# A table of biases built in the first half-step, a norm's small products moved into products, and half 0's squares ordered behind an inverse root

## The chip, the cores and the metric

The kernel runs on one core of one Trainium2 chip. The core has TensorE (PE, matrix products), VectorE (DVE), ScalarE (ACT), GpSimd (POOL) and SyncE (SP, which issues transfers); 16 DMA engines move data between HBM and the on-chip memory. The metric is the device time of one execution in microseconds (us), lower is better; a time given for a kernel is the median of several runs. A profile is taken from one further execution.

## The reference

One step of a decoder layer on 544 tokens of width 1024 (512 of a prompt, 8 samples of 4): a SwiGLU half-step, a mixer of two groups of heads (RWKV-7 and differential attention), and a second SwiGLU half-step, each between two norms. The attention adds a bias that depends on the distance of two tokens alone, looked up in a table of 32 buckets for 4 heads.

```python
def layer(x, l, shift0, wkv0, attend, P):
    g = P['norm_gains'][l]
    h = x + 0.5 * rms_norm(swiglu(rms_norm(x, g[0], NORM_EPS), P['ff1_in'][l], P['ff1_out'][l]), g[1], NORM_EPS)
    m, k, v, wkv, shift = mixer(rms_norm(h, g[2], NORM_EPS), l, shift0, wkv0, attend, P)
    h = h + rms_norm(m, g[3], NORM_EPS)
    h = h + 0.5 * rms_norm(swiglu(rms_norm(h, g[4], NORM_EPS), P['ff2_in'][l], P['ff2_out'][l]), g[5], NORM_EPS)
    return h, k, v, wkv, shift
...
    s = jnp.einsum('bqhmd,bkhmd->bhmqk', q, k).astype(jnp.float32) * (A_QK_DIM ** -0.5)
    s = s + bias[None, :, None]
```

## The kernel before

The tokens lie along the free dimension in two halves of 272 (half 0 and half 1, index s), the 1024 features in 8 blocks of 128 partitions (KB). A product in fp32 is made of three products in a faster type: every matrix is kept as a high part and a low part, and the three are high by high, low of x by high of w, high of x by low of w. `weights` (L110 to L125) brings one block of weights: SyncE loads it into a buffer named wraw (there are three, shared by all loads of this kind), ScalarE copies the high part whi (L118), and the low part wlo is either a subtraction on VectorE (L124) or, with `added`, a negated copy on ScalarE (L121) and a transfer on GpSimd's queue that adds the weights onto it (L122).

`dot` multiplies a block of weights with one half of x: for eight blocks k the two products with whi (L144, L145), then eight with wlo (L153). `opening` (L345 to L373) makes the first products of a stage: for half 0 with `dot`, then for half 1, two weights at a time, with `mm3` (L129, L130, L131). While these run, the stage before is being closed: `close_half` (L293 to L327) makes the residual h of a half (L301, L302 on VectorE), splits it into xh (ScalarE, L279) and xl (VectorE, L281), the operands of the products, and adds up its squares for the next norm (ScalarE L259, VectorE L260). The norm itself is a list of steps: small products that sum the squares (L191), an inverse root of 9 small VectorE instructions (L216 to L226), small products that spread it over the partitions (L238), and for the next norm a copy of it, rpre (L291), by which results are scaled (for the mixer, L741). `dot` and `opening` issue one step each when their products are through, so `norm` and `ends`, the two lists, set where the small products stand in TensorE's order.

The scheduler of the tile layer orders instructions on each engine by priority; `tc.issue_after(ins)` sets one behind another, and `tc.high_priority()` sets it ahead of others that are ready.

The mixer's opening is followed by the gates: a Tanh and a Sigmoid (L807, L808) on the first two projections, their split parts twh, twl, sgh, sgl, and small products with the weights lora (`gates`, L129 to L131 again). Then come four blocks b=0 to 3, each with three more weights and their products. Ahead of these, in the code, stands the table: L828 loads the buckets of 640 distances (oh), L832 multiplies them with the table of biases (tab), L833 negates the result into rb, L836 writes rb to memory, L839 writes it 128 times side by side (rb_d, 1280 KB). Both oh and rb are wraw buffers. The attention reads rb_d at L1130, 634 us into the run.

The half-steps go through 22 blocks of inner features in four groups. The first group opens with `opening` for blocks 0 and 1 and goes on with pairs of blocks from j = 2.

Of the kernel before, what the change touches and what calls it, by code (L numbers as in the profile page):

```python
# [9 lines left out]
FT = mybir.dt.float32  # L10
# [10 lines left out]
KB = DM // 128  # L21
# [31 lines left out]
def build(ctx, tc, A):  # L53
# [84 lines left out]

    def dot(ps, w, xs, k0=0, ins=None):

        n = len(xs)
        for k in range(n):
            hi, _ = wcols(w, k0 + k)
            T.matmul(ps, hi, xs[k][0], start=k == 0, stop=False)  # L144
            latest[0] = T.matmul(ps, hi, xs[k][1], start=False, stop=False).ins  # L145
        rest = norm and norm[0] is None
        if rest:
            norm.pop(0)
        elif norm:
            ins = norm_step(latest[0], norm)  # L150
        with after(ins):
            for k in range(n):
                latest[0] = T.matmul(ps, wcols(w, k0 + k)[1], xs[k][0], start=False, stop=k == n - 1).ins  # L153
        if rest and norm and norm[0] is not None:
            norm_step(latest[0], norm)
# [21 lines left out]
    def xbank():  # L177
        return px.tile([128, 512], FT, name="pb")

    turn, last, latest = [0], [None], [None]  # L180

    def acc_tile():
        turn[0] += 1
# [19 lines left out]
    def inv_sqrt(pt, n, scale=1.0, eps=None, least=None, y=None):  # L203


        if y is None:
            v, y, t = [wk.tile([128, n], FT, name=nm, bufs=3, padded_shape=[128, 24]) for nm in ("rv", "ry", "rt")]
        else:
            v, t = [wk.tile([128, n], FT, name=nm, tag="sq") for nm in ("wv", "wt")]
        src, dst = pt[:], v  # L210
        if len(src.shape) == 2:
            src = src[:, :n]
        else:
            dst = v.rearrange("p (b j e) -> p b j e", j=src.shape[2], e=src.shape[3])
        if least is None:
            V.tensor_scalar(dst, src, 0.5 * scale, 0.5 * eps, op0=OP.mult, op1=OP.add)  # L216
        else:
            V.tensor_scalar(dst, src, least, 0.5, op0=OP.max, op1=OP.mult)
        V.tensor_scalar(y.bitcast(I32), v.bitcast(I32), -0.5, MAGIC, op0=OP.mult, op1=OP.add)
        V.tensor_tensor(t, v, y, op=OP.mult)  # L220
        V.tensor_tensor(t, t, y, op=OP.mult)
        V.scalar_tensor_tensor(t, t, -5 / 3, t, op0=OP.add, op1=OP.mult)
        V.scalar_tensor_tensor(y, t, 1.25, y, op0=OP.add, op1=OP.mult)
        V.tensor_tensor(t, v, y, op=OP.mult)
        V.scalar_tensor_tensor(t, t, -3.375, y, op0=OP.mult, op1=OP.mult)
        V.scalar_tensor_tensor(y, t, 2.25, y, op0=OP.add, op1=OP.mult)  # L226
        return y

    def spread(y, e, bank=bank):
# [65 lines left out]
    def close_half(h, s, y, sq, gcol, pre=None, xp=None, spill=None, out=None):  # L295

        drain()

        def residual(r, m):
            t = wk.tile([128, HALF], FT, name="pn")  # L300
            V.scalar_tensor_tensor(t, y[s][m], gcol[:, m:m + 1], r, op0=OP.mult, op1=OP.mult)  # L301
            (G if out is not None and m in (0, 2, 4) else V).tensor_tensor(h[s][:, m], h[s][:, m], t, op=OP.add)  # L302
            if out is not None and (m % 2 or m == KB - 2):
                q = m if m >= KB - 2 else m - 1
                nc.sync.dma_start(out[s, :, q:m + 1], h[s][:, q:m + 1])
            if pre is not None:
                pre.split(xp, h, s, m)
            if spill is not None and m % 2:
                nc.scalar.dma_start(spill[s, :, m - 1:m + 1], h[s][:, m - 1:m + 1])

        def steps(r):
            for m in range(KB):
                with (tc.high_priority() if s else ExitStack()):
                    residual(r, m)
                yield
            if pre is not None:
                for m in range(KB):
                    pre.sq[s].add(h[s][:, m])
                    yield

        if s == 1 and pre is not None:
            norm.extend((lambda _: inverses(sq), lambda iv: later.append(steps(spread(iv, 1))),
                         None, None, lambda _: inverses(pre.sq[0]), lambda iv: pre.scale(0, iv)))
            ends.extend((lambda _: inverses(pre.sq[1]), lambda iv: pre.scale(1, iv)))
        else:
            later.append(steps(rstd(sq)))
# [17 lines left out]
    def opening(ws, xs, take, n=4):  # L344


        for i, w in enumerate(ws):
            ps = acc_tile()
            dot(ps, w, xs[0])
            take(0, i, ps)  # L350
            tick(4)
        drain()
        for i in range(0, len(ws), n):
            banks = [acc_tile() if j < 3 else abank()[:, :HALF] for j in range(min(n, len(ws) - i))]
            for k in range(KB):
                for w, ps in zip(ws[i:i + n], banks):
                    latest[0] = mm3(ps, wcols(w, k), xs[1][k], k == 0, k == KB - 1)
                if norm and k == 2:
                    norm_step(latest[0], norm)
            if ends and i:  # L360
                norm_step(latest[0], ends)
            for j, ps in enumerate(banks):
                take(1, i + j, ps)
        norm.extend(ends)
        ends.clear()
# [59 lines left out]

        return sets, scaled(), mixtures()

    def ff(win, wout, pre, h, done, xp, end, lead=(), begin=None, ahead_of_end=None):
        with ExitStack() as st:
            pool = lambda n, to=st, **kw: to.enter_context(tc.tile_pool(name=n, bufs=1, reuse_waits="tile", **kw))  # L430
            yp, fa = pool("ffy"), pool("fa")
# [110 lines left out]
            for gi, (j0, j1) in enumerate(GROUPS):  # L542
                if gi == 0:
# [16 lines left out]
                    scaled_raw(0)  # L560
                    behind = [None, None]
                    for j in range(2, j1, 2):
                        ws = [[weights(win[i, n], 1024, added=begin is None and j == 2) for n in range(2)] for i in (j, j + 1)]
                        for s in range(2):
                            for both in ws:
                                pg, pu = acc_tile(), acc_tile()
# [91 lines left out]
        pre.scale(1)  # L658

    hd = dram.tile([2, 128, KB, HALF], FT, name="h_d")  # L660
    mix_in = Pre(2)
    mixp = []

# [11 lines left out]
    def ff1_end():  # L675
# [1 line left out]
        again(A["x"])  # L677

    ff(A["ff1_in"], A["ff1_out"], pre, h,
       lambda s, y, sq: close_half(h, s, y, sq, hgains[:, 1, :], mix_in, mixp[0], hd), xp, ff1_end, lead, begin, mix_weights)  # L680
    xs, rs = mix_in.xs, mix_in.rs
    h_stack.close()

# [139 lines left out]
            out.append(t)  # L823
        return out


    oh = wp.tile([33, NRB], FT, name="wraw", bufs=3)
    nc.sync.dma_start(oh, A["rbkt"])  # L828
    rb = wp.tile([AH, NRB], FT, name="wraw", bufs=3)
    for c0, c1 in ((0, 512), (512, NRB)):  # L830
        ps = abank()
        T.matmul(ps[:AH, :c1 - c0], tab, oh[:, c0:c1], start=True, stop=True)  # L832
        V.tensor_scalar(rb[:, c0:c1], ps[:AH, :c1 - c0], -1.0, None, op0=OP.mult)  # L833

    rb_1 = dram.tile([AH, NRB], FT, name="rb_1")
    nc.sync.dma_start(rb_1, rb)  # L836
    rb_d = dram.tile([128, AH * NRB], FT, name="rb_d")
    src = rb_1[0:1]
    nc.sync.dma_start(rb_d, bass.AP(tensor=src.tensor, offset=src.offset, ap=[[0, 128], [1, AH * NRB]]))  # L839
    for b in range(4):  # L840
        cat = pp.tile([128, NCH, 5, CH], FT, name="cat", bufs=2)
        if b:
# [794 lines left out]
```

## Time and profile before

| what | value |
|---|---|
| timed runs | 1208.91, 1209.03, 1210.56 us |
| median | 1209.03 us |
| profiled execution | 1214.19 us, its span 1212.4 us |
| granted TensorE clock, mean over the span | 0.982 |
| TensorE busy | 1173.4 us, 97% of the span |
| VectorE, ScalarE, GpSimd busy | 816.1, 587.9, 165.0 us |

The span is the time between the first and the last instruction in the record. The granted clock is the share of full speed that TensorE had. A busy share near 100% says that an engine nearly always has work, not that it works at full speed.

### The profile page before, as it was taken

What the parts mean: (1) busy time and instruction counts of PE and PEld (TensorE: products, weight loads), DVE (VectorE), ACT (ScalarE), POOL (GpSimd) and SP (SyncE); (2) the same over time, 40 slices, a digit from 0 to 9 for tenths busy, and PEclk for the clock granted to TensorE, in tenths of its full rate; (3) what the DMA queues carried; (4) which work ended last, traced back from release to release, by engine and by line L of the source; (5) the groups of instructions that cost most, each with busy time, mean ns of one, the idle gap of its engine ahead of it and who ended that gap; (6) DMA issues with size and microseconds to landing.
All of it is one profiled execution on the core that took longest, in us unless ns stands there. A gap on an engine that the chain in (4) does not pass through costs nothing. (4 is left out here: it accounts for less than half of the span.)

```text
span 1212.4 us, 25438 instructions
## 1 busy us (share of the span) xinstructions
PE 1173.4 (97%) x10020; PEld 1106.2 (91%) x10020; DVE 816.1 (67%) x1876; ACT 587.9 (48%) x1085; POOL 165.0 (14%) x227
## 2 busy tenths in 40 slices
PE   8999999999999979989999999999999999999996
PEld 8999999999999969989897645998999999999995
DVE  7794684865866657768525458785783766857856
ACT  6455552644645465543214446576455544625530
POOL 0001210110102055531000021101002110101001
PEclk8999999999999979999999899999999999999998
DMA  6328884875756277789426376663538985867532
GB/s 217 101 67 240 213 210 128 209 182 143 166 193 158 76 203 206 218 228 251 116 66 194 140 283 216 210 181 110 136 95 236 219 200 141 212 155 169 122 124 74
DMA packets 86349, 206.47 MB, mean 170 GB/s; under 512 B 9137, under 2 KB 20145, under 8 KB 84822
## 3 DMA queue, kind: packets, MB, share of 16 engines
q1 hardware_dynamic: 66150, 151.10, 37.4%
q0 software_dynamic: 17776, 49.29, 23.2%
q10 hardware_dynamic: 2304, 4.46, 1.0%
q8 instruction: 79, 1.29, 0.4%
q14 instruction: 40, 0.33, 0.1%
HBM read 187.17 MB, written 18.95 MB: 170 GB/s over the span
## 5 line engine op out<-in xcount | busy, mean ns | idle before, releaser
L118 ACT ACTIVATE whi<-wraw 128x1024 fp32r<-128x1024 f32 (+2 forms) x127 | 116.8, 923 | 166.8 <-PE mm L145 70.4
L144 PE MATMUL mm<-xh,whi 128*128 128x272 f32 x456 | 122.7, 299 | 11.5 <-ACT whi L118 7.7
L145 PE MATMUL mm<-xl,whi 128*128 128x272 f32 x456 | 121.3, 295 | 0.0
L124 DVE TENSOR_TENSOR wlo<-wraw,whi 128x1024 fp32r<-128x1024 f32 (+2 forms) x98 | 98.2, 1004 | 17.7 <-ACT whi L118 14.4
L144 PEld LDWEIGHTS mm<-xh,whi 128*128 128x128 f32 x456 | 88.7, 195 | 13.3 <-ACT whi L118 8.0
L463 POOL DMA_DIRECT2D t<-in_ff_in_dram x32 | 38.6, 1205 | 397.3 <-DMA t<-in_ff_in_dram 207.8
L145 PEld LDWEIGHTS mm<-xl,whi 128*128 128x128 f32 x456 | 88.8, 195 | 0.4 <-DVE xl L281 0.3
L509 DVE TENSOR_TENSOR ga<-pb,ga 128x272 f32<-128x272 f32 x140 | 61.1, 436 | 22.3 <-PE pb L498 20.1
L153 PE MATMUL mm<-xh,wlo 128*128 128x272 f32 x456 | 70.1, 293 | 1.4 <-DMA wlo<-in_ff_in_dram 1.4
L495 PE MATMUL pb<-sh,t1h 128*128 128x272 f32 x256 | 66.7, 288 | 0.0
L496 PE MATMUL pb<-sl,t1h 128*128 128x272 f32 x256 | 66.6, 287 | 0.0
L608 DVE TENSOR_TENSOR y<-mm,y 128x272 f32<-128x272 f32 x66 | 29.0, 440 | 54.9 <-PE mm L153 54.5
L153 PEld LDWEIGHTS mm<-xh,wlo 128*128 128x128 f32 x456 | 62.0, 191 | 2.2 <-DMA wlo<-in_ff_in_dram 1.8
L145 PE MATMUL mm<-hd1l,whi 128*128 128x272 f32 x242 | 62.7, 289 | 1.0 <-DVE hd1l L165 1.0
L145 PE MATMUL mm<-hd0l,whi 128*128 128x272 f32 x242 | 62.6, 288 | 0.0
L144 PE MATMUL mm<-hd0h,whi 128*128 128x272 f32 x242 | 62.2, 288 | 0.0
L144 PE MATMUL mm<-hd1h,whi 128*128 128x272 f32 x242 | 62.1, 289 | 0.0
L144 PE MATMUL pb<-xh,whi 128*128 128x272 f32 x232 | 60.9, 292 | 0.6 <-ACT whi L118 0.6
L145 PE MATMUL pb<-xl,whi 128*128 128x272 f32 x232 | 59.7, 288 | 0.0
L475 ACT ACTIVATE t1h<-t 128x1024 fp32r<-128x1024 f32 x32 | 33.9, 1061 | 52.6 <-issue 26.5
L495 PE MATMUL pb<-fa,whi 128*128 128x272 f32 x216 | 56.2, 288 | 0.0
L496 PE MATMUL pb<-fa,whi 128*128 128x272 f32 x216 | 56.2, 288 | 0.0
(508 smaller groups left out, 3621.0 us busy)
## 6 DMA issues: line engine op xcount, KB each, us to landing
wraw<-in_ff_in_dram SPq DMA_DIRECT2D x55, 512.0 KB, 5.3
wlo<-in_ff_in_dram POOLq DMA_DIRECT2D x36, 512.0 KB, 7.4
t<-in_ff_in_dram SPq DMA_DIRECT2D x64, 256.0 KB, 3.7
t<-in_ff_in_dram POOLq DMA_DIRECT2D x32, 512.0 KB, 5.9
wraw<-in_w_in_dram SPq DMA_DIRECT2D x26, 512.0 KB, 7.3
wlo<-in_w_in_dram POOLq DMA_DIRECT2D x25, 512.0 KB, 9.0
wraw<-in_ff_out_dram SPq DMA_DIRECT2D x32, 384.0 KB, 3.0
wraw<-in_ff_out_dram SPq DMA_DIRECT2D x32, 320.0 KB, 3.2
```

The source lines that it names most:

```text
L118: S.activation(hi, raw, AF.Copy)
L124: V.tensor_tensor(lo, raw, hi.bitcast(FT), op=OP.subtract)
L144: T.matmul(ps, hi, xs[k][0], start=k == 0, stop=False)
L145: latest[0] = T.matmul(ps, hi, xs[k][1], start=False, stop=False).ins
L153: latest[0] = T.matmul(ps, wcols(w, k0 + k)[1], xs[k][0], start=False, stop=k == n - 1).ins
L463: G.dma_start(t1, bass.AP(tensor=src.tensor, offset=src.offset, ap=[[1024, 128], [128 * 1024 + 512, 2], [1, 512]]), accum_op=OP.add)
L475: S.activation(hi, src, AF.Copy)
L495: T.matmul(ps, c, x[k][0], start=k == 0, stop=False)
L496: T.matmul(ps, c, x[k][1], start=False, stop=False)
L509: V.tensor_tensor(dst, p, q, op=op)
L608: V.tensor_tensor(y[s][m], ps, y[s][m], op=OP.add)
```

## The change

Four things change. The table is built by a function `distances`, called in the first half-step, with tiles of its own and its three transfers on GpSimd's queue. `dot` issues a step of a norm after the fourth of its eight blocks k, and sets the products after that behind the step; `opening` does the like for the list `ends`. Half 0's squares leave the steps of half 0 and are queued by the step that makes half 1's sums and root, behind the last instruction of that root. In the second half-step's first group the accumulating transfer makes the low parts of block 3 alone, no longer those of blocks 2 and 3.

```diff
     def dot(ps, w, xs, k0=0, ins=None):
-        n = len(xs)
-        for k in range(n):
-            hi, _ = wcols(w, k0 + k)
-            T.matmul(ps, hi, xs[k][0], start=k == 0, stop=False)
-            latest[0] = T.matmul(ps, hi, xs[k][1], start=False, stop=False).ins
+        n, then = len(xs), None
         rest = norm and norm[0] is None
         if rest:
             norm.pop(0)
-        elif norm:
-            ins = norm_step(latest[0], norm)
+        for k in range(n):
+            hi, _ = wcols(w, k0 + k)
+            with after(then):
+                T.matmul(ps, hi, xs[k][0], start=k == 0, stop=False)
+                latest[0] = T.matmul(ps, hi, xs[k][1], start=False, stop=False).ins
+            if k == 3 and norm and not rest:
+                then = ins = norm_step(latest[0], norm)
...
-        V.scalar_tensor_tensor(y, t, 2.25, y, op0=OP.add, op1=OP.mult)
+        root[0] = V.scalar_tensor_tensor(y, t, 2.25, y, op0=OP.add, op1=OP.mult).ins
...
-            if pre is not None:
-                for m in range(KB):
-                    pre.sq[s].add(h[s][:, m])
-                    yield
+            if pre is not None and s:
+                yield from squares(1)
+
+        def squares(i, ins=None):
+            for m in range(KB):
+                with after(ins):
+                    pre.sq[i].add(h[i][:, m])
+                yield
+
+        def first(_):
+            iv = inverses(sq)
+            later.append(squares(0, root[0]))
+            return iv
 
         if s == 1 and pre is not None:
-            norm.extend((lambda _: inverses(sq), lambda iv: later.append(steps(spread(iv, 1))),
+            norm.extend((first, lambda iv: later.append(steps(spread(iv, 1))),
...
-            if ends and i:
-                norm_step(latest[0], ends)
+                if ends and i >= n and k == 3:
+                    norm_step(latest[0], ends)
...
+                        if midway and j == 4:
+                            midway()
-                        ws = [[weights(win[i, n], 1024, added=begin is None and j == 2) for n in range(2)] for i in (j, j + 1)]
+                        ws = [[weights(win[i, n], 1024, added=begin is None and i == 3) for n in range(2)] for i in (j, j + 1)]
...
+    rb_d = dram.tile([128, AH * NRB], FT, name="rb_d")
+    def distances():
+        dp = h_pool("dist")
+        oh = dp.tile([33, NRB], FT, name="oh")
+        nc.gpsimd.dma_start(oh, A["rbkt"])
+        rb = dp.tile([AH, NRB], FT, name="rb")
+        for c0, c1 in ((0, 512), (512, NRB)):
+            ps = abank()
+            T.matmul(ps[:AH, :c1 - c0], tab, oh[:, c0:c1], start=True, stop=True)
+            V.tensor_scalar(rb[:, c0:c1], ps[:AH, :c1 - c0], -1.0, None, op0=OP.mult)
+        rb_1 = dram.tile([AH, NRB], FT, name="rb_1")
+        nc.gpsimd.dma_start(rb_1, rb)
+        src = rb_1[0:1]
+        nc.gpsimd.dma_start(rb_d, bass.AP(tensor=src.tensor, offset=src.offset, ap=[[0, 128], [1, AH * NRB]]))
```

The same lines of the table leave the mixer, where they stood with oh and rb as wraw buffers and with `nc.sync` in place of `nc.gpsimd`.

SyncE's order before, from the weights of the gates on (lora is their load, w_in are the mixer's weights):

```order
L793 DMA wraw<-in_lora_dram 128x1024
L828 DMA wraw<-in_rbkt_dram 33x640
L115 DMA wraw<-in_w_in_dram 128x1024 x2
L836 DMA rb_5596<-wraw 4x640
L839 DMA rb_d<-rb_5596 128x2560
L115 DMA wraw<-in_w_in_dram 128x1024 x6
L911 DMA cat_d<-cat 128x2560
```

And now:

```order
L823 DMA wraw<-in_lora_dram 128x1024
L115 DMA wraw<-in_w_in_dram 128x1024 x10
L927 DMA cat_d<-cat 128x2560
L907 DMA bon_d<-bon 128x544
L900 DMA bon_d<-bon 128x544
```

The three transfers of the table are gone from this place, and the loads of weights stand in one row, two of the ten from further back.

TensorE's order before, at the end of the mixer's opening (sgl is the low part of the opening's fifth weight, L238 the third group of spread products, and the products of xh_0 with whi are the first of the next weights):

```order
L129 MATMUL mm<-xh_7_5281,sgh 128x272
L130 MATMUL mm<-xl_7_5283,sgh 128x272
L131 MATMUL mm<-xh_7_5281,sgl 128x272
L238 MATMUL pb<-cst,ry 128x128 x3
L832 MATMUL pb<-wraw,tab 4x512
L832 MATMUL pb<-wraw,tab 4x128
L144 MATMUL pb<-xh_0_4798,whi 128x272
L145 MATMUL pb<-xl_0_4800,whi 128x272
```

And now:

```order
L129 MATMUL mm<-xh_4_5318,sgh 128x272
L130 MATMUL mm<-xl_4_5320,sgh 128x272
L239 MATMUL pb<-cst,ry 128x128 x3
L131 MATMUL mm<-xh_4_5318,sgl 128x272
L129 MATMUL mm<-xh_5_5325,sgh 128x272
L130 MATMUL mm<-xl_5_5327,sgh 128x272
L131 MATMUL mm<-xh_5_5325,sgl 128x272
```

The table's two matmuls are gone, and the spread stands ten products ahead of the opening's end. The first product of the gates (twh with lora_h) stood 32 products behind the spread, and stands 77 behind it now.

VectorE's order before, around half 1's inverse root in the mixer's opening (L260 with sqa_5043 are half 0's squares, y_0 and h_4514 are of half 1):

```order
L260 TENSOR_TENSOR sqa_5043<-sqa_5043,sq 128x272 x2
L281 SCALAR_TENSOR_TENSOR xl_6_5011<-h_4512,gains,xh_6_5009 128x272
L281 SCALAR_TENSOR_TENSOR xl_7_5040<-h_4512,gains,xh_7_5038 128x272
L260 TENSOR_TENSOR sqa_5043<-sqa_5043,sq 128x272 x4
L216 TENSOR_SCALAR rv<-pb 128x3
L260 TENSOR_TENSOR sqa_5043<-sqa_5043,sq 128x272
L219 TENSOR_SCALAR ry<-rv 128x3
```

And now, from the end of the root on:

```order
L226 SCALAR_TENSOR_TENSOR rt<-rt,ry 128x3
L227 SCALAR_TENSOR_TENSOR ry<-rt,ry 128x3
L261 TENSOR_TENSOR sqa_5164<-sqa_5164,sq 128x272 x3
L302 SCALAR_TENSOR_TENSOR pn<-y_0_194,hgains,pb 128x272
L302 SCALAR_TENSOR_TENSOR pn<-y_1_195,hgains,pb 128x272
L261 TENSOR_TENSOR sqa_5164<-sqa_5164,sq 128x272
L303 TENSOR_TENSOR h_4531<-h_4531,pn 128x272 x2
L261 TENSOR_TENSOR sqa_5164<-sqa_5164,sq 128x272
```

Half 0's squares stood ahead of the root, and now they stand behind it, between the residuals of half 1. On TensorE the sums for this root stand about 19 products nearer to the start of the opening, and its spread comes 28 products behind them where it came 39 behind. In the first half-step the table's two matmuls now stand behind the first norm's sums (L288) and ahead of the third weight's products for half 0.

## Rows read from the trace of the kernel before

**Rows 1.** Windows: us, busy (and count) by engine, clock, DMA share, GB/s

```profile
425.00:435.90 10.90, 4.62 (x30) 3.24 (x29) 7.34 (x18) 6.20 (x10) 8.71 (x19) 0.82 0.33 92
435.90:438.80 2.90, 2.87 (x12) 2.87 (x13) 2.31 (x3) 2.66 (x4) 2.90 (x7) 0.50 0.86 237
438.80:443.70 4.90, 3.23 (x27) 2.75 (x26) 3.16 (x8) 1.11 (x2) 2.90 (x9) 0.85 0.92 304
443.70:452.80 9.10, 9.10 (x40) 8.60 (x40) 3.29 (x10) 8.99 (x11) 1.72 (x2) 0.52 1.05 268
25.00:35.00 10.00, 10.00 (x82) 10.00 (x81) 8.01 (x18) 7.18 (x16) 0.00 (x0) 1.00 0.09 20
```

**Rows 2.** Timeline of TensorE, 425 to 444: start, us, what, [idle before <- releaser]

```profile
425.69 0.49 PE L238 MATMUL pb<-cst,ry 128*128 128x128 f32 x3
426.11 1.24 PE L832 MATMUL pb<-wraw,tab 33*4 33x512 f32 x4
...
435.93 0.60 PE L144 MATMUL mm<-xh,whi 128*128 128x272 f32 x1 [6.03 <-ACT whi L118]
...
443.70 0.59 PE L144 MATMUL mm<-xh,whi 128*128 128x272 f32 x1 [1.67 <-ACT whi L118]
```

**Rows 3.** Timeline of ScalarE, 432 to 443

```profile
432.31 0.66 ACT L807 ACTIVATE xr<-xr 64x544 f32<-64x544 f32 x1 [3.78 <-DVE xr L764]
...
434.84 1.04 ACT L118 ACTIVATE whi<-wraw 128x1024 fp32r<-128x1024 f32 x1
...
436.73 0.64 ACT L164 ACTIVATE twh<-xr 128x544 fp32r<-128x544 f32 x1
...
442.59 1.06 ACT L118 ACTIVATE whi<-wraw 128x1024 fp32r<-128x1024 f32 x1 [4.03 <-DMA wraw<-in_w_in_dram]
```

**Rows 4.** Timeline of SyncE's queue, 410 to 460

```profile
415.80 11.91 SPq L115 DMA_DIRECT2D wraw<-in_w_in_dram  x2
...
433.68 24.82 SPq L115 DMA_DIRECT2D wraw<-in_w_in_dram  x6
```

**Rows 5.** Windows, columns as in rows 1 (TensorE, its weight loads, VectorE, ScalarE, GpSimd)

```profile
16.00:20.00 4.00, 3.72 (x28) 3.29 (x27) 3.92 (x10) 4.00 (x9) 0.00 (x0) 1.00 0.44 164
404.00:416.00 12.00, 10.30 (x73) 9.16 (x73) 11.97 (x41) 8.04 (x22) 0.00 (x0) 1.00 0.25 93
660.00:680.00 20.00, 17.86 (x179) 11.25 (x178) 5.53 (x21) 6.42 (x25) 0.00 (x0) 0.74 0.19 62
825.00:840.00 15.00, 13.34 (x101) 12.47 (x100) 12.67 (x40) 9.52 (x22) 0.00 (x0) 1.00 0.20 75
845.00:863.00 18.00, 15.95 (x122) 15.05 (x121) 9.84 (x25) 9.64 (x19) 1.44 (x2) 1.00 0.74 190
```

**Rows 6.** Timeline of GpSimd, 840 to 841

```profile
840.38 0.88 POOL L122 DMA_DIRECT2D wlo<-in_ff_in_dram  x1 [60.92 <-ACT wlo L121]
```

**Rows 7.** Timeline of VectorE, 401 to 438

```profile
401.73 0.91 DVE L301 SCALAR_TENSOR_TENSOR pn<-y,hgains,pb 128x272 f32<-128x272 f32 x2 [3.34 <-PE pb L238]
...
406.14 0.43 DVE L260 TENSOR_TENSOR sqa<-sqa,sq 128x272 f32<-128x272 f32 x1
...
430.59 0.87 DVE L833 TENSOR_SCALAR wraw<-pb 4x512 f32<-4x512 f32 x2
...
437.41 2.37 DVE L165 TENSOR_TENSOR twl<-xr,twh 128x544 fp32r<-128x544 f32 x1
```

**Rows 8.** Timeline of TensorE, 18 to 20

```profile
19.16 0.39 PE L144 MATMUL pb<-xh,whi 128*128 128x272 f32 x1 [0.28 <-ACT whi L118]
```

**Rows 9.** Timeline of SyncE's queue, 8 to 12

```profile
8.70 0.33 SPq L648 DMA_DIRECT2D shin<-in_shift_dram  x1
10.26 0.34 SPq L649 DMA_DIRECT2D tab<-in_table_dram  x1
```

**Rows 10.** DMA issues, 0 to 40: KB each, median us from issue to landing

```profile
shin<-in_shift_dram SPq DMA_DIRECT2D x1, 56.0 KB, 8.6
```

**Rows 11.** Page, groups of instructions: count, busy us, mean ns, idle before, releaser

```profile
L124 DVE TENSOR_TENSOR wlo<-wraw,whi 128x1024 fp32r<-128x1024 f32 (+2 forms) x98 | 98.2, 1004 | 17.7 <-ACT whi L118 14.4
```

More of the change, by code (lines that the diff above doesn't have):

```diff
@@ L178, in xbank @@
         return px.tile([128, 512], FT, name="pb")
-    turn, last, latest = [0], [None], [None]
+    turn, last, latest, root = [0], [None], [None], [None]
     def acc_tile():
@@ L426, in combined, with ff @@
         return sets, scaled(), mixtures()
-    def ff(win, wout, pre, h, done, xp, end, lead=(), begin=None, ahead_of_end=None):
+    def ff(win, wout, pre, h, done, xp, end, lead=(), begin=None, midway=None, ahead_of_end=None):
         with ExitStack() as st:
@@ L679, in build @@
     ff(A["ff1_in"], A["ff1_out"], pre, h,
-       lambda s, y, sq: close_half(h, s, y, sq, hgains[:, 1, :], mix_in, mixp[0], hd), xp, ff1_end, lead, begin, mix_weights)
+       lambda s, y, sq: close_half(h, s, y, sq, hgains[:, 1, :], mix_in, mixp[0], hd), xp, ff1_end, lead, begin, distances, mix_weights)
     xs, rs = mix_in.xs, mix_in.rs
@@ L824, in gates @@
         return out
[L827 to L839, printed above, removed]
     for b in range(4):
```

## The prediction, written before the changed kernel ran

> **What bounds the kernel now.** First I read the windows around the places that the diff touches: TensorE is busy nearly all the time elsewhere (82 products in 10.00 us of work in a quiet stretch, 0.122 us apart [rows 1]), so the total is TensorE's work plus the stretches where it waits or runs at the lower clock. The largest such stretch that the diff touches is the end of the mixer's opening and the first gates: in 425.0 to 435.9 TensorE is busy 4.62 of 10.90 us, and behind it come two stretches at a granted clock of 0.50 and 0.52, half of the full 2.4 GHz [rows 1]. Then TensorE's own order of events there: the third group of spread products (L238) at 425.69, the table's products (L832, 1.24 us), one weight's 16 products, then 6.03 us of waiting for the ScalarE copy of the next weight (L118), and at 443.70 another 1.67 us for the next copy [rows 2]. Then what those copies wait for. The first, at 434.84, stands on ScalarE behind the Tanh and Sigmoid of the gates, which themselves waited 3.78 us for VectorE; the second, at 442.59, waited 4.03 us for its raw weight [rows 3]. SyncE's queue shows why the raw weight is late: two loads took 11.91 us to issue from 415.80, and the next six only start at 433.68 [rows 4]. Between them the queue has the table's small transfers, and the table's two tiles hold two of the three wraw buffers.
>
> The other stretches are the two openings and what follows the second: in 404 to 416 TensorE is busy 10.30 of 12.00 us, in 825 to 840 (the opening of the second half-step) 13.34 of 15.00, in 845 to 863 15.95 of 18.00 [rows 5]. In the openings VectorE, which makes half 1's low parts, is busy almost without a break (11.97 of 12.00 and 12.67 of 15.00 us) and TensorE waits for it; in the last stretch it has time to spare (9.84 of 18.00), and what comes late are accumulating transfers of low weights, which GpSimd issues from 840.38 on [rows 5, 6].
>
> **The change part by part.** The sum is made against the profiled execution of 1214.19 us (span 1212.4); the median of the three timed runs, 1209.03, is 5.16 lower, and I carry the difference over unchanged.
>
> *The table leaves the mixer.* Three things go. (1) The idle time: 10.90-4.62 = 6.28, and 4.90-3.23 = 1.67 in 438.8 to 443.7, with 0.03 between: 7.98 us [rows 1]. (2) The half-speed time behind the two gaps: 12 products in 2.87 us and 40 in 9.10, against 0.122 each at full clock: (2.87-1.46)+(9.10-4.88) = 5.6 us [rows 1]. (3) The table's products, 1.24 us [rows 2]. Whether the idle time really goes depends on two suppliers. Raw weights: the slots are no longer taken by table tiles, so the three loads behind lora go out as earlier copies free a slot, up to 12 us sooner than now [rows 4]. ScalarE: its weight copies now stand ahead of the Tanh. And the order changed so that 77 products lie between the third spread and the first lora product, where now 32 do. Their cover is 77 x 0.122 = 9.4 us. The gates need, from the spread to the high part twh: 425.69 to 436.73+0.64 = 11.7 us now [rows 2, 3], less VectorE's 0.87 us at L833 [rows 7] and less the two weight copies between Sigmoid and twh (434.84 to 436.73, 1.9 us): 8.9. So twh is in time by half a microsecond. The low part twl ends at 437.41+2.37 = 439.78 now [rows 7], 14.1 us behind the spread, less the same 2.8 = 11.3, and its first product comes 88 products behind the spread, 10.7 us. That may leave a wait of 0.6 us. I take out all 13.6 us of (1) and (2), and put in new waits of 2.4 us for b=0 and b=1 together. The bounds of these are 0 (both covers hold) and 6.3 (one wait with a clock drop, priced below). I take a value nearer to the low end, since both covers are within a microsecond of what is needed.
>
> *The table enters the first half-step.* Its matmuls come right behind the norm's sums, where TensorE is at 1.00 clock and busy 3.72 of 4.00 us [rows 5]; they cost 1.24 and swallow the wait of 0.28 that stands there now [rows 8], so 1.0. VectorE's two negations (0.87 [rows 7]) come ahead of the norm's chain, of which perhaps a third shows; oh's 84 KB join the loads of the start, 0.3 us at 268 GB/s [rows 1]. In sum -1.5, between -1.0 (only the products) and -4 (the table tab landing late: it is issued at 10.26, and shin, issued 1.6 us before it, took 8.6 us, so near 19, when it is needed [rows 9, 10]). The broadcast of 1280 KB comes into a stretch with a DMA share of 0.09 [rows 1] and is read at 634 us only; it costs nothing there. If that cover were gone, 1280 KB at the 268 GB/s of 443.7 to 452.8 [rows 1] are 4.9 us of the queue, and a weight load behind it would be as late. The Trainium skill, "DMA: Bandwidth & Descriptors", section "Issuing engines are not separate DMA queues", says that transfers from GpSimd and SyncE run on the same 16 engines and interleave, so the move to another queue would by itself hide nothing; by that the move gains only through the slots and through the idle stretch.
>
> *Steps in the middle of products, and half 0's squares behind the root.* In the first opening VectorE, done with half 1's inverse root, stands 3.34 us before L301 at 401.73 for the spread [rows 7]. Now the sums come about 19 products earlier, and 28 in place of 39 products lie between sums and spread: some 30 x 0.122 = 3.6 us earlier, which removes the 3.34. But half 0's eight squares, which VectorE did before the root, now fall into half 1's chain: 0.43 each [rows 7], and four of them before the low parts that TensorE waits for: 1.7 us. So the chain is about 1.6 us earlier in place of 3.3, against waits of 12.00-10.30 = 1.70 [rows 5]; the first of these (the high part) stays. I take 1.2, between -1 (all eight squares ahead of the low parts, 3.4, and the spread only 2.4 us earlier) and 1.7. In the second half-step's opening the structure is the same and 1.66 us stand idle [rows 5], a third of it for other things; I take 1.0, between -1 and 1.7.
>
> *Two weights by VectorE in place of accumulating transfers.* The first accumulating transfer is issued at 840.38, when ScalarE's copy is there [rows 6]; TensorE later waits for such weights, 18.00-15.95 = 2.05 us in four places [rows 5]. Now two of the four are subtracted on VectorE, which has 8.2 us free in that stretch, against 1.0 each (98.2 us for 98) [rows 11], and the other two land earlier for it. I take 2.0, between 0 and 2.05.
>
> Sum: 13.6 + 1.2 + 1.2 + 1.0 + 2.0 - 1.5 - 2.4 = 15.1. The profiled run would be 1199.1, and the median 1209.0-15.1 = 1193.9, say 1194.
>
> **The rivals.** *A new wait in b=0 or b=1.* A wait of about 2 us costs more than itself: in 660 to 680, 2.14 us of idle time stand with a mean clock of 0.74 [rows 5]; that is 10.4 us at half speed, of which 8.3 were work, and half of that, 4.1, is lost: 6.3 in all. For it: the margins of 0.5 and -0.6 us, and DMA shares of 0.9 to 1.05 in 438.8 to 452.8 [rows 1] when low parts must land. Against: the largest transfer of that stretch, the table's broadcast, is gone. One such wait gives 1194+6.3-2.4 = 1198, two 1204.
>
> *The stall only moves.* If the gates' chain on VectorE and GpSimd sets the time of block b=0, then the 13.6 come back in front of lora, and what remains is 1.2+1.2+1.0+2.0-1.5 = 3.9: 1205. With half of the openings' gains gone too it is 1207, within 0.2%. For it: TensorE gets to lora only 0.5 us after twh. Against: in the trace ScalarE's two copies lie between the Sigmoid and twh, and they are gone from there.
>
> *The table late at the start (slower).* The table's products stand in TensorE's order before all of the following products; if oh or tab is not there, TensorE stands at 18.9. To eat the 15.1 us a wait of 11.0 plus 4.1 for the clock is enough; from 13.4 us on (oh landing at 32) it is slower by over 0.2%; a landing at 35 gives 1214. For it: oh is now GpSimd's transfer in a time when VectorE is busy 3.92 of 4.00 us [rows 5]. Against: it is the first thing on its queue, 18 us ahead of its use, and the DMA share falls to 0.44 by then. The Trainium skill, "DMA: Bandwidth & Descriptors", section "SWDGE vs HWDGE vs iDMA", has a rule that speaks for it: GpSimd builds descriptors in software in SBUF, and VectorE in its two-port mode locks it out of that. No row shows a GpSimd transfer held up by VectorE here; by the rule oh would come some time later, up to this rival's case.
>
> *The steps don't move.* The order shows the sums and spreads earlier, but if waits on other engines set them, the openings give 0 and the time is 1196; the forecast's range holds it.
>
> **How the numbers follow.** Forecast 0.53, with its own range 1189 to 1198; a new wait 0.27 (1198 to 1204); the stall moves 0.13 (1203 to 1208); the table late 0.04 (over 1209); the steps don't move 0.03. A range from 1187 (all covers hold, openings at their upper bounds) to 1206 leaves under 2 in 10 out. 0.2% is 2.4 us, about what a measurement of this kernel can tell from no change: faster is below 1206.6. Faster: 0.53+0.27+0.03 and some 0.05 to 0.1 of the 0.13: 0.89. Within: 0.06; slower: 0.05.
>
> **What would show it.** Right: no wait for L118 over 1 us between the third spread and the second block, a clock of 1.00 from there to the third; the table's products at 19 us with less than 1 us before them; VectorE's wait before L301 gone in both openings; TensorE's waits for low weights at 848 to 859 under 0.5 us in sum. Wrong: a wait before the first lora product or for a low weight with a clock of 0.5 behind it (first or second rival); TensorE idle before the table's products (third); waits for low parts of half 1 as long as now (the squares).

## The result and the profile after

The changed kernel takes 1194.69 us (median of four runs, 1194.13 to 1195.31) where the kernel before takes 1209.80 beside it (four runs, 1208.91 to 1212.38): a ratio of 0.987, interval 0.986 to 0.989. The forecast was 1194. Two later runs of the kernel before, at 1424.65 and 2132.42 us, fell into a slower state of the chip and are left out of every figure below.

Windows of the changed kernel, with the columns of [rows 1], at the places that answer to [rows 1] (the second and third line) and [rows 5] (the first and the last three), and around two stretches more:

```profile
402.00:414.00 12.00, 10.66 (x82) 9.94 (x81) 10.04 (x36) 8.34 (x19) 0.52 (x1) 1.00 0.18 70
424.00:434.00 10.00, 10.00 (x80) 9.70 (x79) 8.71 (x18) 4.96 (x10) 8.73 (x20) 1.00 0.85 220
434.00:444.00 10.00, 10.00 (x80) 9.54 (x79) 8.58 (x19) 8.76 (x13) 7.12 (x13) 1.00 0.01 2
452.80:459.60 6.80, 6.56 (x71) 5.81 (x70) 5.85 (x14) 2.94 (x7) 4.47 (x9) 1.00 1.05 277
459.60:466.40 6.80, 6.80 (x29) 6.30 (x29) 4.41 (x16) 4.05 (x6) 1.27 (x1) 0.50 0.53 213
476.70:483.50 6.80, 6.80 (x73) 6.00 (x72) 5.47 (x8) 5.00 (x9) 5.96 (x9) 1.00 1.03 356
483.50:490.30 6.80, 6.80 (x30) 6.30 (x29) 5.07 (x18) 3.88 (x5) 3.11 (x5) 0.50 1.05 277
660.00:680.00 20.00, 19.28 (x284) 13.31 (x284) 10.91 (x46) 10.14 (x34) 0.00 (x0) 1.00 0.62 212
811.00:826.00 15.00, 14.52 (x118) 14.28 (x117) 13.44 (x40) 9.95 (x23) 0.00 (x0) 1.00 0.24 82
831.00:849.00 18.00, 18.00 (x146) 18.00 (x146) 12.23 (x29) 8.49 (x18) 0.88 (x1) 1.00 0.50 125
```

The 20 us behind the mixer's opening, where TensorE stood idle for 6.28 us and then ran at half speed [rows 1], are busy without a gap and at full clock. The second half-step's opening has 0.48 us of idle time left, and the stretch behind it none. But two stretches at a clock of 0.50 have come in at 459.6 and 483.5, and TensorE is busy there all the time: 29 and 30 products in 6.80 us. No wait stands in them; the two ahead of the first are 0.78 us at 446 and 0.24 at 453.8.

TensorE's timeline of the changed kernel, at five places:

```profile
17.17 1.24 PE L684 MATMUL pb<-oh,tab 33*4 33x512 f32 x4
...
422.81 0.49 PE L239 MATMUL pb<-cst,ry 128*128 128x128 f32 x3
...
446.02 0.88 PE L239 MATMUL pb<-cst,rx 128*128 128x128 f32 x6 [0.78 <-DVE rx L234]
...
458.18 1.50 PE L192 MATMUL pb<-cst,ksq 128*128 128x2 f32 x12
...
654.88 1.13 PE L1013 MATMUL pb<-ar,kbv 64*128 64x128 f32 x8 [1.65 <-DMA kbv<-cat_d]
```

The table's products run at 17 us without a wait. The two transfers that they need landed, by the view of DMA issues (KB, us from issue to landing), so:

```profile
oh<-in_rbkt_dram POOLq DMA_DIRECT2D x1, 82.5 KB, 3.5
tab<-in_table_dram SPq DMA_DIRECT2D x1, 0.5 KB, 7.2
```

The first wait behind the mixer's opening (whose third spread is at 422.81) is 0.78 us, in block b=0. The twelve two-column sums at 458.18 stand right ahead of the first stretch at half speed.

To see where time came and went I numbered TensorE's 10020 products in either kernel by their start and put the same numbers side by side. "Lead" is the start in the profile of the kernel before less the start here, in us. From product 74 to 3288 it holds 0.5 us that are no gain: the table's four products (two matmuls, four in the record) are counted at 71 to 74 here and at 3289 to 3292 before. From 3300 on the numbers match again, and the 1.24 us that the table's products took in the kernel before lie between 3100 and 3300.

| up to product number | what lies before it | before, us | after, lead | after, second profile (e9), lead |
|---|---|---|---|---|
| 100 | start | 23.0 | 1.3 | 0.8 |
| 3100 | first half-step | 399.7 | 1.4 | 0.9 |
| 3300 | mixer's opening | 428.7 | 3.3 | 2.9 |
| 3450 | end of the opening, first gates | 461.5 | 16.8 | 15.9 |
| 4200 | blocks b=0 to 3 | 549.1 | 8.6 | 10.4 |
| 5700 | RWKV and attention | 660.2 | 8.6 | 9.8 |
| 5850 | the wait for kbv | 678.7 | 13.6 | 12.0 |
| 7100 | attention, mixer's end | 827.9 | 14.6 | 12.0 |
| 7240 | second half-step's opening | 848.2 | 16.7 | 14.1 |
| 7400 | blocks 2 and 3 there | 870.7 | 19.2 | 16.6 |
| 10019 | end | 1202.8 | 19.4 | 16.7 |

The two profiles differ by 19.1 us (spans 1212.4 and 1193.3), the medians by 15.1: the profiled run of before, 1214.19, lay above the median.

### The profile page after: what moved, and what is told of

The parts are those of the page before. It is cut to its first block, busy times and chain, and to the rows that moved or that the text cites. A ratio compares the mean times of both kernels' runs of the same rounds, so it can differ in the third digit from the quotient of the medians.

```text
span 1193.3 us, 25431 instructions
## 1 busy us (share of the span) xinstructions
PE 1166.6 (98%) x10020; PEld 1103.5 (92%) x10020; DVE 821.2 (69%) x1878; ACT 583.6 (49%) x1081; POOL 169.5 (14%) x228
## 5 line engine op out<-in xcount | busy, mean ns | idle before, releaser
L118 ACT ACTIVATE whi<-wraw 128x1024 fp32r<-128x1024 f32 (+2 forms) x127 | 116.8, 923 | 164.3 <-PE mm L149 75.3
L124 DVE TENSOR_TENSOR wlo<-wraw,whi 128x1024 fp32r<-128x1024 f32 (+2 forms) x100 | 100.6, 1008 | 17.7 <-ACT whi L118 16.7
```

The costliest lines, as they stand in the source:

```text
L118: S.activation(hi, raw, AF.Copy)
L124: V.tensor_tensor(lo, raw, hi.bitcast(FT), op=OP.subtract)
```

## The experiments

Twelve experiments ran; e9 is the changed kernel once more, and e12 is e11 once more. Each ratio is to the kernel before, timed beside it at medians of 1211.2 to 1212.1 us; the changed kernel's is 0.987.

**e1, the table back.** The changed kernel, with `distances` and its call removed and the old lines of the mixer put back (its edit is the part of the diff on the table, backwards).

```diff
+    oh = wp.tile([33, NRB], FT, name="wraw", bufs=3)
+    nc.sync.dma_start(oh, A["rbkt"])
+    rb = wp.tile([AH, NRB], FT, name="wraw", bufs=3)
...
+    nc.sync.dma_start(rb_1, rb)
...
+    nc.sync.dma_start(rb_d, bass.AP(tensor=src.tensor, offset=src.offset, ap=[[0, 128], [1, AH * NRB]]))
     for b in range(4):
```

> The changed kernel with the table alone put back into the mixer (its tiles in wraw buffers, its transfers on SyncE's queue). If the table's place among the raw weight loads made the stall behind the mixer's opening, TensorE waits 5 to 8 us again for the copies L118 before the first blocks, and the time is 1198 to 1204: the waits and the slow clock behind them (13.5 us) come back, and the two falls of the clock at 460 and 484 us, which cost the changed kernel 8.6 us there, go. If the earlier norm steps and the moved squares took the stall away, there is no such wait and the time stays within 1.5 us of 1194.7.

1200.88 us, 0.992 (0.989 to 0.995). TensorE's waits of this kernel, 420 to 450 us (who waited for whom, total, times, longest):

```profile
PE mm L148 <- ACT whi L118: 2.7, 1, 2.7
PE pb L129 <- ACT twh L165: 1.1, 1, 1.1
PE pb L148 <- DVE pr L753: 1.0, 1, 1.0
PE mm L154 <- DMA wlo<-in_w_in_dram: 1.0, 1, 1.0
```

The wait for L118 is back, but as 2.7 us and not the 6.03 of [rows 2], and the lead at product 3450 is 7.1 us. So the table does make the stall, and the earlier steps and moved squares alone also take away about half of it. I had not counted that: the sum gave this stall to the table alone. The two falls of the clock at 460 and 484 us are gone here, as expected (another of 6.8 us has come in at 427.1, behind the table's products and the wait of 1.1):

```profile
440.00:460.00 20.00, 16.04 (x138) 14.60 (x139) 13.41 (x34) 10.80 (x15) 9.54 (x15) 1.00 1.05 304
460.00:480.00 20.00, 20.00 (x159) 19.33 (x158) 14.48 (x39) 10.97 (x13) 7.99 (x17) 1.00 0.58 147
480.00:500.00 20.00, 20.00 (x181) 19.11 (x180) 12.89 (x34) 11.64 (x17) 10.18 (x18) 1.00 0.87 237
```

**e2, the table alone.** The kernel before with `distances` as in the changed kernel, nothing else; where it is called:

```diff
                     for j in range(2, j1, 2):
+                        if midway and j == 4:
+                            midway()
```

> The kernel before with the table alone moved to the first half-step. If the table made the stall, the 6.03 and 1.67 us of waiting are gone and the time is 1200 to 1205, since the openings and the accumulating transfers of the second half-step are as before (some 7 us of the gain are missing). If the norm steps took the stall away, it is still there, and the time is 1208 to 1211.

1204.38 us, 0.993 (0.990 to 0.995). The lead at 3450 is 12.4 us, with one wait left between 420 and 450 us:

```profile
PE mm L153 <- DMA wlo<-in_w_in_dram: 1.4, 1, 1.4
```

The table's place is enough for most of this stall; the gains of table and steps overlap and don't add.

**e3, tiles of its own.** The kernel before, the table where it was, on SyncE's queue.

```diff
-    oh = wp.tile([33, NRB], FT, name="wraw", bufs=3)
+    oh = pq.tile([33, NRB], FT, name="oh")
...
-    rb = wp.tile([AH, NRB], FT, name="wraw", bufs=3)
+    rb = pq.tile([AH, NRB], FT, name="rb")
```

> The kernel before with the table where it was, on SyncE's queue, but with tiles of its own in place of two of the three wraw buffers. If the buffers were the fault, this alone gives what moving the table gives: no wait over 1 us for L118 in the first blocks, and a time within 1.5 us of the kernel with the table alone moved. If its place in the queue or on TensorE was the fault, the waits stay and the time is 1207 to 1211.

1204.09 us, 0.994 (0.990 to 0.997). Windows of this kernel at the place of [rows 1]:

```profile
425.00:436.00 11.00, 11.00 (x83) 9.85 (x82) 8.18 (x19) 5.64 (x11) 7.90 (x17) 1.00 0.99 251
436.00:447.00 11.00, 11.00 (x86) 10.24 (x85) 9.95 (x26) 9.84 (x14) 8.32 (x18) 1.00 0.38 121
```

The stall is gone with the table still in place: no idle time in 22 us, and a lead of 13.6 us at product 3450 where it was 0.2 at 3300. It was the two raw weight buffers, neither the queue nor the table's matmuls.

**e10, the same in the changed kernel.** The edit of e3 on e1's kernel.

> The changed kernel with the table back in the mixer and on SyncE's queue, but with tiles of its own in place of two raw weight buffers. If the buffers alone made the table's part of the stall, there is no wait over 1 us for L118 between 420 and 450 us, and the time is within 1.5 us of the changed kernel's. If the early place matters for itself (its matmuls, its transfers among the weight loads), waits of 2 us or more stand there and the time is 1198 or more.

1196.47 us, 0.987 (0.985 to 0.989), with the changed kernel at 1195.19 beside it. The waits between 420 and 450 us:

```profile
PE pb L129 <- ACT twh L165: 0.9, 1, 0.9
PE pb L192 <- ACT ksq L873: 0.4, 1, 0.4
PE pb L130 <- DVE twl L166: 0.2, 1, 0.2
```

Once the table has tiles of its own, its place makes 1.3 us between the medians, which is less than the spread of either kernel (1193.6 to 1198.1 and 1192.6 to 1202.8) and so not shown to cost anything.

**e5, four accumulating transfers again.** The changed kernel with the old rule for the second half-step.

```diff
-                        ws = [[weights(win[i, n], 1024, added=begin is None and i == 3) for n in range(2)] for i in (j, j + 1)]
+                        ws = [[weights(win[i, n], 1024, added=begin is None and j == 2) for n in range(2)] for i in (j, j + 1)]
```

> The changed kernel with the accumulating transfers of block 2 put back in the second half-step (four on GpSimd's queue again). If they made the waits there, TensorE waits again about 2 us for low weights between 830 and 845 us and the time is 2 to 2.5 us longer than the changed kernel's, 1196 to 1198. If the earlier norm steps took the waits away, they do not come back and the time stays at 1194 to 1195.5.

1200.84 us, 0.993 (0.990 to 0.996), more than the 1196 to 1198 expected. Its waits, 825 to 860 us:

```profile
PE mm L154 <- DMA wlo<-in_ff_in_dram: 2.7, 2, 2.3
PE pb L154 <- DMA wlo<-in_ff_in_dram: 1.6, 1, 1.6
```

4.3 us of waiting in place of the 2.05 of the kernel before. The opening ahead of it is shorter here, so TensorE comes to the transfers earlier and waits longer: it is ready for the first of these low weights 16.4 us earlier than in the kernel before (831.02 against 847.46), while the four transfers are issued between 16.1 and 15.1 us earlier. From product 7100 to 7400 this kernel's lead falls from 14.6 to 14.1, where the changed kernel's rises by 4.6. Without this edit the second opening's gain is given back in the next stretch.

**e6, half 0's squares in their old place; e7, the steps at the ends of products.**

```diff
-            if pre is not None and s:
-                yield from squares(1)
+            if pre is not None:
+                yield from squares(s)
...
-            later.append(squares(0, root[0]))
```

```diff
-            if k == 3 and norm and not rest:
-                then = ins = norm_step(latest[0], norm)
+        if norm and not rest:
+            ins = norm_step(latest[0], norm)
...
-                if ends and i >= n and k == 3:
-                    norm_step(latest[0], ends)
+            if ends and i:
+                norm_step(latest[0], ends)
```

> The changed kernel with half 0's squares left in the steps of half 0, as before. My sum counted their place behind the root as a cost of 1.7 us in VectorE's chain of each opening: then this kernel waits less for half 1's low parts and the time is 1192 to 1194. If the squares ahead of the root hold the root back, its spread comes later, TensorE's waits for the low parts grow by 1 to 1.5 us in each opening and the time is 1196 to 1198.

> The changed kernel with the norm's steps at the ends of products again. If the earlier steps gave the openings their gain, TensorE waits there 1 us longer each, and the time is 1196.5 to 1198; the stall behind the mixer's opening stays away, since the table is out of the raw weights' buffers. If the steps also carry the first blocks, a wait for twh or a copy L118 of 1 us or more appears there and the time is over 1199.

1201.15 us, 0.990 (0.987 to 0.993), and 1201.37, 0.991 (0.988 to 0.993). In the mixer's opening (395 to 425 us) both wait for half 1's low parts as the changed kernel does not; of e6 and e7 the line reads the same, and the changed kernel's stands below it:

```profile
PE mm L130 <- DVE xl L282: 1.5, 3, 1.0
```

```profile
PE mm L130 <- DVE xl L282: 0.5, 2, 0.3
```

Over this opening (products 3100 to 3300) the lead of e6 grows by 0.2 us, that of e7 by 0.9, and that of the changed kernel by 2.0. Some 0.75 us of each are the table's (1.24 us for its products in the kernel before, 0.5 for four ordinary ones here), which leaves -0.6, 0.2 and 1.2 for the opening itself. From 7100 to 7400 e6 and e7 gain 3.6 and 2.7, against 4.6. So both edits are needed for the openings, by one profile of each. That the squares go behind the root is a gain of 1.8 and 1.0 us there, not the cost of 1.7 that I put into the sum. The intervals of both ratios overlap the changed kernel's, so the times alone do not settle what either edit is worth. Some 3 us of the 6 that either loses are the openings' and the first blocks' (e7 waits 1.8 us there for low weights); the rest, in these profiles, are stretches at half speed at 582, 657 and 661 us that the changed kernel's first profile doesn't have.

**e4, e8, e9, e11, e12: the new stretches at half speed.** These asked why the clock falls at 459.6 and 483.5 in a TensorE that never stands idle. The 16 small products of cat (L924, 32 in the record) stood ahead of both falls. e4 orders each block's small products behind the next block's spread; e8 makes them one dense product in two blocks, and so leaves out part of the RWKV state. Their edits, cut to the lines that matter:

```diff
+    waiting = []
...
         kk = rn
+        if waiting:
+            waiting.pop(0)()
...
-        ps = abank()
-        for c in range(NCH):
...
+        def strips(b=b, cat=cat):
+            ps = abank()
+            with after(last[0]):
+                for c in range(NCH):
...
+        waiting.append(strips)
+        if b > 1:
+            waiting.pop(0)()
```

```diff
-        for c in range(NCH):
+        if b < 2:
+            T.matmul(ps, C["heads"], cat[:, :, 1, :], start=True, stop=True)
+        for c in range(NCH if b > 1 else 0):
...
+        if b < 2:
+            V.tensor_scalar(ltm[:, b * NCH:(b + 1) * NCH], c64(ps), 0.0, None, op0=OP.mult)
```

> The changed kernel, with the 16 small products of each block's cat (64 by 64) ordered behind the next block's spread, so that they no longer stand right ahead of the gates' products and the two-column sums. If it is this row of small products (3.4 us in which few columns pass) that lets the granted clock fall to 0.50 at 460 and 484 us, the clock stays at 1.00 from 425 to 500 us and the time is 1187 to 1190. If the falls come from the short waits ahead of them (0.78 us at 446, 0.24 at 453.8) or from transfers, the clock falls as before and the time is 1193 to 1197.

> The changed kernel, but in blocks 0 and 1 the 16 small products of cat (64 by 64) are one product of 128 rows and 512 columns, whose result is multiplied by zero (so that part of the RWKV state is left out). If the row of small products lets the clock fall, no stretch at 0.50 lies between 455 and 495 us and the time is 1187 to 1190. If the falls have another cause, they are there in the profile and the time is 1193 to 1197.

1194.16 us, 0.986 (0.983 to 0.989), and 1195.56, 0.987 (0.985 to 0.989). Windows of e4, then of e8:

```profile
455.00:462.00 7.00, 7.00 (x51) 6.37 (x50) 5.47 (x12) 5.31 (x10) 4.99 (x9) 0.99 1.05 310
462.00:465.40 3.40, 3.40 (x17) 3.40 (x17) 1.69 (x8) 0.69 (x2) 0.77 (x1) 0.51 0.66 266
```

```profile
485.50:488.90 3.40, 3.40 (x16) 3.15 (x15) 2.23 (x7) 2.83 (x4) 1.27 (x1) 0.51 0.85 298
505.90:509.30 3.40, 3.40 (x14) 3.12 (x14) 2.32 (x7) 3.18 (x5) 3.10 (x6) 0.50 1.06 282
```

The clock still falls, a shorter time and elsewhere, and the times are the changed kernel's. My theory fell: the small products of cat are not what the falls need. (Ahead of the fall at 505.9, in a block that e8 leaves as it was, they do stand, 5 us back.) Whether they help to make a fall longer is open. What still stands ahead of each of these is the gates' products and the two-column sums L192. But first e9, the changed kernel unaltered:

> The changed kernel once more, unaltered, for a second profile and more times beside the next two. If where the clock falls belongs to the program, it falls again near 460 and 484 us for 6.8 us each and the times lie within 1194 to 1196. If it hangs on where the start of a run lies, as the times of the kernel before suggest (1208 to 1219 us, at mean clocks of 0.991 to 0.978), the falls stand elsewhere and the times spread by 5 us or more.

1195.19 us (1192.63 to 1202.77), 0.987 (0.984 to 0.990). Windows of its profile:

```profile
461.20:464.60 3.40, 3.40 (x16) 3.15 (x15) 2.90 (x10) 2.44 (x4) 1.27 (x1) 0.50 0.70 283
481.70:488.50 6.80, 6.80 (x30) 6.30 (x29) 4.77 (x18) 4.09 (x5) 3.31 (x5) 0.50 1.06 270
655.80:659.20 3.40, 3.40 (x30) 2.12 (x28) 2.17 (x6) 1.04 (x6) 0.00 (x0) 0.50 0.01 2
```

The same program falls at nearly the same places but for other lengths, once more at 656, and its times spread over 10 us. The Trainium skill, "TensorE: Matmul & The Clock Gate", section "What's actually happening", says that the default state of the clock is the lower one, which activity releases, and that the watch on activity runs freely and does not start with the kernel. The runs fit that but do not test it: within these blocks the place is the program's, and how long the clock falls, at 656 also whether it falls, changes from run to run.

Then the sums. Each takes 128 columns in place of 2 (the heads matrix whole; two of the columns are used, so the result is the same):

```diff
-        pt = bank()
+        parts = []
         for s, hs in enumerate(halves):
-            sums(pt[:, s * 6:], [sq[:, hs]], heads2)
-        iv = inv_sqrt(pt, 12, least=1e-24)
+            pt = bank()
+            sums(pt, [sq[:, hs]], C["heads"])
+            parts.append(pt[:, :384].rearrange("p (j e x) -> p j e x", j=3, e=2)[:, :, :, 0])
+        iv = inv_sqrt(None, 12, least=1e-24, parts=parts)
```

The rest of the edit lets `inv_sqrt` read the two halves from `parts`, with one VectorE instruction each.

> The changed kernel, but the twelve two-column sums of each block's squares (L192) are made with 128 columns each; the result is the same, of the columns two are used. They stand right ahead of each fall of the clock that I have seen between 440 and 490 us. If it is these that let the clock fall, it stays at 1.00 from 440 to 495 us, and the time is 3 to 6 us under that of the changed kernel in the same call, less some 1.5 us for the wider products. If not, it falls there as before and the time is 1 to 3 us over it.

> The kernel with the wide sums once more, for a second profile, since the falls of the clock move from run to run. If the two-column sums are what lets it fall between 455 and 495 us, there is again no fall there, as in the first profile of this kernel and unlike all nine profiles of kernels with the narrow sums and without the stall (a fall at 460 to 467 us or at 481 to 488 us in each). If the first was luck, one stands there. The median tells whether it beats the changed kernel: under 1193 it does, over 1196 it does not.

1198.06 us, 0.987 (0.983 to 0.990), and 1192.39, 0.985 (0.981 to 0.988). Windows of e12, then two of e11:

```profile
440.00:460.00 20.00, 19.26 (x173) 18.54 (x173) 17.54 (x46) 12.04 (x18) 13.94 (x27) 1.00 0.74 188
460.00:480.00 20.00, 20.00 (x172) 18.63 (x170) 15.27 (x41) 12.44 (x18) 12.89 (x19) 1.00 0.68 225
480.00:500.00 20.00, 20.00 (x177) 19.18 (x176) 14.97 (x40) 10.81 (x15) 9.64 (x14) 1.00 0.65 184
```

```profile
460.00:480.00 20.00, 20.00 (x174) 18.76 (x173) 15.22 (x43) 13.00 (x19) 12.21 (x16) 1.00 0.64 219
...
660.00:680.00 20.00, 19.28 (x230) 13.38 (x223) 9.38 (x40) 9.66 (x32) 0.00 (x0) 0.82 0.61 212
```

In both profiles the clock is 1.00 from 440 to 500 us; in all ten profiles of kernels with narrow sums and without the long stall (the expectation says nine) it falls there. The wide sums cost TensorE 0.1 us more: 1.60 us for twelve in e11, 1.50 in the changed kernel.

```profile
458.63 1.60 PE L192 MATMUL pb<-cst,ksq 128*128 128x128 f32 x12
```

By product 4200 the lead over the kernel before is 13.8 us in e11 and 14.8 in e12, against 8.6 and 10.4. The short wait ahead of the blocks (0.6 and 0.7 us) is there in both, so it is not that wait that lets the clock fall. This bears the theory out, on two profiles, with a limit: narrow sums are not enough. The kernel before and e1 have them too, and their clock is 1.00 from 455 to 500 us. So has the changed kernel's block b=2, at 508.80, and the clock stays up there. In these places 27 to 44 products of 272 columns stand between the small products of cat and the gates' products. But the second block of e3, e5, e6 and e7, with 7 to 12 there, passes without a fall too. What besides the narrow sums a fall takes is open.

As a faster kernel it is not shown. e12's median lies under the 1193 that its expectation asked for. e11's, 1198.06, lies over the changed kernel's 1195.19 beside it, where 3 to 6 us under it, less some 1.5, were expected. Of the twelve runs five lie at 1189.9 to 1190.8, under all ten of the changed kernel (from 1192.6), but the median is 1194.2 against 1194.7. The profiled run of e11, at 1199.04, lost what it won to falls at 652 and 673 us (the last line of the windows); the other long runs have no profile.

## Why the prediction was right, term by term

The number was right within a microsecond, and the largest term and its cause were right. That it came so near is in part luck: the blocks cost 5.8 us more than forecast, and the start, the second half-step and a wait that the change does not touch gave 8.9 more. The sum was also made against a profiled run 4.4 us above the median; the leads in the profile add up to 19.4 us, the medians differ by 15.1. Of the prediction's own signs one failed: the clock is not 1.00 up to the third block.

- *The stall behind the mixer's opening* (13.6 + 1.2 forecast): from product 3300 to 3450, where the numbers match, the lead grew by 13.5 us (13.0 in e9), and the table's 1.24 us are gone between 3100 and 3300. The cause, raw weight buffers held by the table, is shown by e3, where tiles alone remove it. Half of the stall would have gone with the steps and squares too (e1); the sum gave it to one edit.
- *New waits in b=0 and b=1* (-2.4): the step that failed by size. The lead falls by 8.2 us to product 4200 (5.5 in e9), more than the sum's own bound of 6.3. The waits were forecast rightly, 0.78 us and little else, and twh and twl came in time, so the second rival had no part; but the clock falls without a wait of that size. The first rival had a price of this order, with a wait of 2 us as its cause, which was not there. e11 and e12 keep the clock up there and lose 2.4 and 1.7 us, near the 2.4 of the sum.
- *The start* (-1.5): the products cost 1.24 us and swallowed the 0.28, as said. Yet on equal work (the lead less the 0.5 us of the numbering) the changed kernel is 0.8 us ahead at product 100, 0.3 in e9, and e2, with the table at the same place, is 1.0 behind. So the term is not shown: the start spreads by as much from run to run. In the first profile the lead comes mostly from the start's own stretch at half speed, 3.4 us long and 6.8 in that of before. oh and tab were there, and the third rival had no part: oh landed 3.5 us after its issue at 1.30, tab 7.2 after 9.48, both ahead of their use at 17.17, tab by half a microsecond. The sign that was read for this rival, VectorE busy 3.92 of 4.00 us, is from 16 to 20 us; while oh came, from 1.3 to 4.8, VectorE was busy 0.19 of 3.50 us. The rule of the Trainium skill that stood beside that rival ("DMA: Bandwidth & Descriptors", section "SWDGE vs HWDGE vs iDMA") is neither borne out nor refuted: no run here shows a GpSimd transfer held up by VectorE.
- *The mixer's opening* (1.2): 1.2 in both profiles, when the table's part is taken off the 2.0 in the lead. But the working was not right: the squares' part, put in as a cost of 1.7, is a gain: without it the steps give -0.6 in this opening (e6), and the size came out by luck. The wait of VectorE before the first residual, 3.34 in [rows 7], is 0.27:

```profile
397.28 0.91 DVE L302 SCALAR_TENSOR_TENSOR pn<-y,hgains,pb 128x272 f32<-128x272 f32 x2 [0.27 <-PE pb L239]
```

- *The wait for kbv at 660* (nothing): in the profile of before the 2.14 us of idle time were followed by half speed [rows 5]; in the changed kernel 1.65 were not, which gave 5.0 us between 5700 and 5850. The change didn't touch that: in e9 it was 2.2, with a fall, and e5, e6 and e7 have a fall there. It is the chance of a run, and it makes good what the blocks lost.
- *The second half-step* (1.0 + 2.0): 4.6. The two terms are not independent, as e5 shows: transfers left as before would have eaten the opening's gain.

One small sum of the prediction is off: with half of the openings' gains (2.2) gone the second rival comes to 1206.2, not 1207; nothing else hangs on it.

## What to carry to other kernels

A small tile that borrows a buffer from a stream of weight loads can stop the whole stream: look at what holds each buffer while the queue waits, and try a tile of its own first, before moving the work. When a stage gets shorter, look whether the transfers of the next get earlier by as much: if not, its gain can turn into a wait for them, as in e5. And a profile of one run can hold several microseconds of half speed that belong to that run: compare several runs, place by place, before giving a term to an edit.

## What was not expected of the hardware

TensorE's clock fell to 0.50 for 3.4 or 6.8 us while the record shows it busy all the time, with 29 or 30 products in 6.8 us where 56 of 272 columns would fit at 0.122. Between 440 and 510 us it fell behind the gates' products and the two-column sums, in the ten profiles named, and not in two profiles with the same sums 128 columns wide, which took nearly the same time (1.60 against 1.50 us for twelve). Narrow sums alone do not bring a fall: in the kernel before, in e1 and in single blocks of the others they stand at a clock of 1.00. The times of the kernel before spread from 1206.5 to 1218.8 us at mean clocks from 0.991 to 0.978, all of one program.
